# Chains of a gated delta rule that begin with queries and keys, with the values joining later, in a two-block fp32 kernel

## The chip, the core and the metric

The kernel runs on one core of a Trainium2 chip. TensorE (PE) multiplies, VectorE (DVE), ScalarE (ACT) and GpSimd (POOL) do the element-wise work, and SyncE (SP) issues the loads. The metric is the device time of one execution in microseconds (us); the time before is the median of three runs, and the changed kernel is timed in the same way.

## What is computed

Two transformer blocks run one after the other on 256 tokens of width 1024. The first block puts 16 meta tokens in front (272 rows in all), then has a layer with a gated delta rule and a layer with an mLSTM, each followed by a feed-forward part with a short convolution. The second block has a SwiGLU part, three mixers and another SwiGLU part. Only the delta rule is touched here:

```python
proj = h @ w_in
qkv = silu(causal_depthwise_conv(proj[..., :o1], conv_w))      # q 1024, k 1024, v 2048 columns
z = proj[..., o1:o2]                                           # 2048 columns
beta = sigmoid(...); g = -exp(a_log) * softplus(... + dt_bias) # 16 heads each
q = l2_normalize(q) * 128 ** -0.5;  k = l2_normalize(k)        # 8 heads, each serves 2 value heads
a_mat = eye + (k*beta) @ k^T * decay * strict                  # per head and chunk
u, w = solve(a_mat, [v*beta, k*beta*exp(G)])
v_new = u - w @ S;  o = (q*exp(G)) @ S + (q @ k^T * decay) @ v_new
S = S * gt + (k * exp(G_last - G))^T @ v_new                   # state from chunk to chunk
o = rms_norm(o) * silu(z);  out = o @ w_out
```

## The kernel before

Every fp32 product is split: an operand is cast to a high part (`wh`, `xhl`) and the rest (`wl`), and three matmuls are summed into a PSUM tile `ps`. A projection of 256 columns is 48 such matmuls over 272 tokens. The delta rule's layer has 16 projections for queries, keys and values in four groups (`gdn_proj`: keys, queries, two tiles of values for each group) and 8 projections `z`, 1152 matmuls in all. ACT empties each `ps` into `cx` and `cy`, and DVE runs the four-tap convolution as three instructions on `cy` (`conv4`). PSUM has two buffers for `ps`.

The rest of the layer is a chain for each pair of heads (8) and each of two chunks of 128 tokens, in four lanes at a time. `unit_kq` turns keys and queries to token rows (`kqp`), scales them to unit length with a short row of small DVE instructions (`rq_v`, `rq_y`, `rq_a`), ACT writes `kqtok`, and PE turns them back (shown as `kqp<-eye,kqtok`, called the back transposes below). `gdn_pre` builds the decays (`dp`, `BA`, `kk`) and, in the kernel before, the values as token rows times beta (`vp`, `bv`). `gdn_core` inverts a 128x128 triangular matrix in six doubling levels (`rtp`, then `yp` and `w` by turns, then `zp` and `r2p`; its tile is `RT`), and then forms `up`, `sp` and `op`, the state and the output. After four cores of a group the outputs are normed on DVE (`rq_o`, `on`) and turned by PE (`otp`). The last 16 tokens of all heads are one more chain (`gdn_tail`), which ends in `rsp`, in `r` and in the products `og` that the output projection reads.

The gates (`gdn_gates`: `psba`, `bap`, `lp`, `gg`, `gp`, `stk`, `rp`) are needed by every chain's decays. `residual` turns the input by 24 transposes `trx`.

A planner in the kernel (`Threads`) writes out the order of PE's instructions: each piece of work is a Python generator which yields the tiles and PSUM banks that its next step needs, or an event, and a number that is added as a wish for a later time. The planner keeps an estimated clock and always takes the first generator whose step is ready. PE runs exactly that order. The order on DVE, ACT and POOL comes from the scheduler of the tile framework. An engine executes its own list strictly in order, so an instruction that has to wait holds up all that stands behind it.

In the kernel before, the chunk-0 generator runs the gates first and then, group by group, `before(g, 0)`; the chunk-1 generator runs `before(g, 1)`. `before` waits for `proj_done[g]`, all four projections of the group. The functions that the change touches, and what calls them:

Of the kernel before, what the change touches and what calls it, by code (L numbers as in the profile page):

```python
# [208 lines left out]
class Kern:  # L209
# [664 lines left out]
    def residual(self):  # L874

        for k in range(KD):
            yield [f"p{k % 4}", 10.0 + 1.0 * k]
            self.lane = k % 4
            p = self.plane("trx", (128, T))
            for t, (o, P) in enumerate(TT):  # L880
                self.tr(p[:, o:o + P], self.xt[t][k // 4][:P, (k % 4) * 128:(k % 4) * 128 + 128], P)
            self.A.copy(self.hs[k], p[:])
# [107 lines left out]

    def gdn_proj(self, X, g):
        W = self.i["gdn_w_in"][0]
        qs, ks, v0, v1 = (self.vslot() for _ in range(4))
        for base, dst in ((1024 + g * 256, ks), (g * 256, qs), (2048 + g * 512, v0), (2304 + g * 512, v1)):
            yield from self.linear_g(W, base, 256, KD, X, T, lambda m, p: self.conv4(p, base // 128 + m, dst[:, m, :]))
        tl = slice(256, T)
        self.G.tensor_copy(self.kqtail[:, 0, 2 * g:2 * g + 2, :], ks[:, :, tl])
        self.G.tensor_copy(self.kqtail[:, 1, 2 * g:2 * g + 2, :], qs[:, :, tl])
        for n, v in enumerate((v0, v1)):
            self.G.tensor_copy(self.vtail[:, 4 * g + 2 * n:4 * g + 2 * n + 2, :], v[:, :, tl])  # L1000
        return qs, ks, (v0, v1)

    def unit_kq(self, x, c):


        n = len(x)
        yield list(x) + [f"pu{c}"]
        self.lane = f"u{c}"
        ss = self.tiny([128, n], "kqss")
        p = self.plane("kqp", (128, n, 128))  # L1010
        for h in range(n):
            self.tr(p[:, h, :], x[h])
        for h in range(n):
            self.square_sum(ss[:, h:h + 1], p[:, h, :])
        r = self.rsqrt_small([128, n], ss[:], 1.0, 4 * EPS)
        rq = r[:].rearrange("p (h e) -> p h e", e=2)[:, :, 1]
        self.ts(rq, rq, 128.0 ** -0.5, ALU.mult)
        kq = self.ring(f"kq{c}", "kqtok", (128, n, 128))
        for h in range(n):
            self.act(kq[:, h, :], p[:, h, :], AF.Copy, scale=r[:, h:h + 1])  # L1020
        yield [kq[:], f"pu{c}", 0.8]
        self.lane = f"u{c}"
        p2 = self.plane("kqp2", (128, n, 128))
        for h in range(n):
            self.tr(p2[:, h, :], kq[:, h, :])
        kqT = self.ring(f"kqT{c}", "kqT", (128, n, 128))
        self.A.copy(kqT[:], p2[:])
        return kq, kqT
# [88 lines left out]

    def gdn_pre(self, q, c, kqT, v):


        sl = slice(c * 128, c * 128 + 128)
        h0 = 2 * q
# [11 lines left out]
        BA = yield from self.decays(kqT[:, 0, :], kqT, diff, 0, self.nG[:, c, h0:h0 + 2])  # L1134
        yield [BA[:], f"pu{c}"]
        self.lane = f"u{c}"
# [4 lines left out]
        for h in range(2):  # L1141
            self.act(bv[:, h, :], vp[:, h, :], AF.Copy, scale=self.beta[:, c, h0 + h:h0 + h + 1])
        return BA, bv

    def gdn_core(self, q, c, kq, kqT, BA, bv, ss, state_of):

        h0 = 2 * q
        lane = self.lane = (q % 2) * 2 + c
        R2 = yield from self.wy_inverse(BA[:, 0], 2, 128)
        aT = BA[:, 1]  # L1150
        S_ = self.St[q]
# [164 lines left out]
    def gdn(self, X):  # L1316
# [6 lines left out]
        proj, state = {}, events(8)  # L1323
        proj_done, after_done = events(), events()
        pre, pre_one, core_done = {}, [events() for _ in range(4)], [events() for _ in range(4)]
# [6 lines left out]
        def projections():  # L1332
            todo, nz = list(range(4)), 0
            while todo or nz < 8:
                if todo and (todo[0] < 2 or all(ev.on for ev in pre_done[todo[0] - 2])):
                    g = todo.pop(0)
                    self.lane = None
                    proj[g] = yield from self.gdn_proj(X, g)
                    proj_done[g].set()
# [9 lines left out]
        def before(g, c):  # L1349
            yield proj_done[g]  # L1350
            qs, ks, vs = proj[g]
            for n in (c, 2 + c):
                if g > 1:
                    yield core_done[g - 2][n]
            u = yield from self.unit_kq([t[:, m, ch[c]] for m in range(2) for t in (ks, qs)], c)
            yield gates_done
            for m in range(2):
                j = 2 * g + m - 3
                if j >= 0:
                    yield core_done[j // 2][j % 2 * 2 + c]  # L1360
                kq, kqT = (t[:, 2 * m:2 * m + 2, :] for t in u)
                pre[g, 2 * m + c] = (kq, kqT) + (yield from self.gdn_pre(2 * g + m, c, kqT, vs[m]))
                pre_one[g][2 * m + c].set()
            pre_done[g][c].set()

# [7 lines left out]

        def first_chunks():
            yield from self.gdn_gates(X)
            gates_done.set()
            for g in range(4):
                yield from before(g, 0)
# [49 lines left out]

        self.th.add([lane(n) for n in range(4)] + [first_chunks(), second_chunks(), gating()])
        self.columns(self.convs, PV_GC)  # L1430
# [1017 lines left out]
```

## Time and profile before

| what | value |
| --- | --- |
| median of 3 runs | 1668.59 us (1667.01 to 1671.13) |
| the profiled execution's own time | 1671.11 us |
| its span from first to last instruction | 1669.3 us |
| TensorE busy | 1564.4 us, 94% of the span |
| VectorE busy | 1120.0 us, 67% |
| ScalarE busy | 927.9 us, 56% |
| GpSimd busy | 579.2 us, 35% |
| chain that ended last | PE 68%, DVE 22%, ACT 5%, DMA 3% |
| mean granted TensorE clock | 0.973 |

The shares are averages over the whole kernel. The delta rule's layer is the first quarter of it, up to about 379 us, and there the digits of the busy tenths of DVE are as high as 8 and PE's fall to 7 and 8. From the output projection on PE stands at 9 in most slices. A row of the timeline gives the start, the duration, the engine, the operation with its tiles, and in brackets how long the engine stood idle in front of it and who released it. Ends of matmuls are modelled, so spacing is read from start to start.

### The profile page before, as it was taken

How to read it: one execution, taken by the hardware profiler on the slowest of the kernel's cores; microseconds unless marked ns; L12 is line 12 of the kernel's file. 1: busy time of each engine (PE TensorE's matmuls, PEld its weight loads, DVE VectorE, ACT ScalarE, POOL GpSimd, SP SyncE). 2: the span in 40 equal slices, each digit the busy share in tenths (PEclk: the TensorE clock that was granted, in tenths of full speed). 3: DMA queues.
4: the chain of work that ended last, by engine and by line, in shares of the span. 5: the costliest groups of instructions: out<-in, count | busy, mean ns of one | idle time of the engine just before them, and what ended most of it. 6: DMA issues, size and time to landing. Idle time of an engine off the chain costs nothing.

```text
span 1669.3 us, 31255 instructions
## 1 busy us (share of the span) xinstructions
PE 1564.4 (94%) x11980; PEld 1475.4 (88%) x11980; DVE 1120.0 (67%) x2223; ACT 927.9 (56%) x1877; POOL 579.2 (35%) x535
## 2 busy tenths in 40 slices
PE   8889888899999998999899998999997899999999
PEld 6788778799899997888899998999985789999987
DVE  5788877766888757457877668464659663566643
ACT  4567767655566554446566556454553655564542
POOL 3574555320200002550344441122275548511221
PEclk9799999999999999999999999999998999999999
DMA  5331221226355554335366564566553335656564
GB/s 158 89 89 52 69 64 47 77 90 214 106 178 174 169 175 111 96 115 164 107 185 192 175 185 148 163 199 192 173 166 111 111 93 150 183 164 188 180 189 151
DMA packets 239100, 235.39 MB, mean 141 GB/s; under 512 B 11511, under 2 KB 226407, under 8 KB 238951
## 3 DMA queue, kind: packets, MB, share of 16 engines
q1 hardware_dynamic: 238326, 231.86, 46.4%
q8 instruction: 94, 1.54, 0.4%
q0 software_dynamic: 496, 1.41, 0.4%
q14 instruction: 56, 0.45, 0.1%
q10 hardware_dynamic: 128, 0.13, 0.0%
HBM read 232.32 MB, written 1.05 MB: 140 GB/s over the span
## 4 chain that ended last, share of the span: by engine, by line
PE 68%; DVE 22%; ACT 5%; DMA 3%; issue 2%; POOL 0%; ACTq 0%; POOLq 0%; DVEq 0%
PE ps L190 52%; PE pst L190 5%; DVE cy L190 3%; DVE rq_a L190 3%; ACT wh L190 2%; DVE RT L190 2%; DVE wl L190 1%; DVE rq_y L190 1%; PE memp L190 1%; DMA wraw<-in_ffn_w_up_dram 1%; DVE xn L190 1%; PE rsp L190 1%; DVE on L190 1%; PE w L190 1%; PE up L190 1%
## 5 line engine op out<-in xcount | busy, mean ns | idle before, releaser
L190 PE MATMUL ps<-xhl,wh 128*128 128x256 f32 (+2 forms) x4496 | 861.6, 294 | 28.9 <-DVE py L190 11.1
L190 PEld LDWEIGHTS ps<-xhl,wh 128*128 128x128 f32 x4496 | 703.0, 193 | 38.3 <-DVE py L190 6.9
L190 ACT CAST wh<-wraw 128x1024 fp32r<-128x1024 f32 (+2 forms) x436 | 448.0, 1029 | 389.8 <-PE ps L190 255.9
L190 PE MATMUL ps<-xhl,wl 128*128 128x256 f32 (+2 forms) x2248 | 626.0, 287 | 0.8 <-DVE wl L190 0.8
L383 POOL TENSOR_TENSOR wl<-wraw,wh 128x512 fp32r<-128x512 f32 (+3 forms) x264 | 334.7, 1291 | 658.2 <-ACT wh L190 622.8
L190 PEld LDWEIGHTS ps<-xhl,wl 128*128 128x128 f32 x2248 | 423.9, 192 | 1.0 <-DVE wl L190 1.0
L190 DVE TENSOR_TENSOR wl<-wraw,wh 128x1024 fp32r<-128x1024 f32 (+2 forms) x237 | 287.4, 1213 | 182.4 <-ACT wh L190 179.2
L190 POOL TENSOR_TENSOR wl<-wraw,wh 128x512 fp32r<-128x512 f32 x134 | 173.9, 1319 | 153.1 <-ACT wh L190 136.2
L190 PE MATMUL ps<-hh,wh 128*128 128x256 f32 (+1 forms) x1056 | 191.1, 283 | 0.0
L190 PEld LDWEIGHTS ps<-hh,wh 128*128 128x128 f32 x1056 | 163.2, 189 | 0.0
L190 PE MATMUL ps<-hh,wl 128*128 128x256 f32 (+1 forms) x528 | 149.7, 284 | 0.0
L190 DVE SCALAR_TENSOR_TENSOR fy<-ps,pvt,fy 128x256 f32<-128x256 f32 (+2 forms) x176 | 84.9, 488 | 25.1 <-ACT fy L190 23.2
L190 PEld LDWEIGHTS ps<-hh,wl 128*128 128x128 f32 x528 | 99.4, 188 | 0.0
L190 DVE SCALAR_TENSOR_TENSOR cy<-cx,pvt,cy 128x271 f32<-128x271 f32 (+2 forms) x96 | 74.5, 779 | 13.5 <-ACT cy L190 12.5
L190 DVE TENSOR_TENSOR hh<-fy,hh 128x256 fp32r<-128x256 f32 (+1 forms) x88 | 64.4, 735 | 13.2 <-ACT hh L190 12.8
L190 POOL MEMSET mvt<- 128x4 f32 x4 | 0.4, 102 | 176.0 <-PE ps L190 176.0
L190 ACT ACTIVATE fy<-ps,pvt 128x272 f32<-128x272 f32 (+1 forms) x88 | 49.5, 568 | 12.3 <-PE ps L190 11.8
L190 DVE TENSOR_TENSOR py<-ps,rstd 128x256 f32<-128x256 f32 x72 | 29.9, 420 | 37.9 <-PE ps L190 37.9
L190 PE MATMUL pst<-wh,hh 128*128 128x512 f32 x176 | 55.1, 394 | 0.0
L190 ACT CAST hh<-fy 128x256 fp32r<-128x256 f32 (+1 forms) x88 | 35.7, 407 | 29.8 <-DVE fy L190 29.0
L190 DVE CAST_PREDICATED RT<-lvl,w 128x512 f16<-128x512 uint8 x67 | 44.9, 683 | 7.1 <-PE w L190 6.8
L190 PE MATMUL ps<-og,wh 128*128 128x272 f32 x256 | 48.6, 289 | 0.1
(523 smaller groups left out, 2420.4 us busy)
## 6 DMA issues: line engine op xcount, KB each, us to landing
wraw<-in_ffn_w_up_dram SPq DMA_DIRECT2D x88, 512.0 KB
wraw<-in_ffn_w_gu_dram SPq DMA_DIRECT2D x88, 512.0 KB
wraw<-in_ffn_w_down_dram SPq DMA_DIRECT2D x79, 512.0 KB
wraw<-in_gdn_w_in_dram SPq DMA_DIRECT2D x48, 512.0 KB
wraw<-in_w_in_dram SPq DMA_DIRECT2D x41, 512.0 KB
wraw<-in_ml_w_in_dram SPq DMA_DIRECT2D x24, 512.0 KB
wraw<-in_gdn_w_out_dram SPq DMA_DIRECT2D x16, 512.0 KB
wraw<-in_ml_w_out_dram SPq DMA_DIRECT2D x8, 512.0 KB
```

The costliest lines, as they stand in the source:

```text
L190: r = f(*args, **kw)
L383: eng.tensor_tensor(l[:, a, b], r[:, a, b], h[:, a, b].bitcast(F32), ALU.subtract)
```

## The change

Keys and queries of a group set an event `kq_done` as soon as their two projections are issued, and `before` waits for that in place of `proj_done`. `gdn_pre` ends with the decays; a new function `gdn_values` makes the value rows, and `gdn_core` waits for them by an event behind its inverse. For group 0 both pairs' decays come first and both pairs' values after them; for later groups values follow each pair's decays. The gates become a generator of their own, in front of the chunk-0 generator, so that the first scaling (group 0, chunk 0, now in the PSUM bank of lane 0) no longer stands behind them. `residual` asks for its transposes later (26 us and 1.5 us apiece, no longer 10 and 1), and no longer names its PSUM bank.

```diff
--- before.py
+++ after.py
@@ -874,7 +874,7 @@
     def residual(self):
 
         for k in range(KD):
-            yield [f"p{k % 4}", 10.0 + 1.0 * k]
+            yield [26.0 + 1.5 * k]
             self.lane = k % 4
             p = self.plane("trx", (128, T))
             for t, (o, P) in enumerate(TT):
@@ -988,11 +988,13 @@
         else:
             self.stt(out, th[:], 1.0, y[:], ALU.add, ALU.mult)
 
-    def gdn_proj(self, X, g):
+    def gdn_proj(self, X, g, kq_done):
         W = self.i["gdn_w_in"][0]
         qs, ks, v0, v1 = (self.vslot() for _ in range(4))
         for base, dst in ((1024 + g * 256, ks), (g * 256, qs), (2048 + g * 512, v0), (2304 + g * 512, v1)):
             yield from self.linear_g(W, base, 256, KD, X, T, lambda m, p: self.conv4(p, base // 128 + m, dst[:, m, :]))
+            if dst is qs:
+                kq_done.set((qs, ks))
         tl = slice(256, T)
         self.G.tensor_copy(self.kqtail[:, 0, 2 * g:2 * g + 2, :], ks[:, :, tl])
         self.G.tensor_copy(self.kqtail[:, 1, 2 * g:2 * g + 2, :], qs[:, :, tl])
@@ -1000,12 +1002,13 @@
             self.G.tensor_copy(self.vtail[:, 4 * g + 2 * n:4 * g + 2 * n + 2, :], v[:, :, tl])
         return qs, ks, (v0, v1)
 
-    def unit_kq(self, x, c):
+    def unit_kq(self, x, c, lane=None):
 
 
         n = len(x)
-        yield list(x) + [f"pu{c}"]
-        self.lane = f"u{c}"
+        lane = f"u{c}" if lane is None else lane
+        yield list(x) + [f"p{lane}"]
+        self.lane = lane
         ss = self.tiny([128, n], "kqss")
         p = self.plane("kqp", (128, n, 128))
         for h in range(n):
@@ -1018,8 +1021,8 @@
         kq = self.ring(f"kq{c}", "kqtok", (128, n, 128))
         for h in range(n):
             self.act(kq[:, h, :], p[:, h, :], AF.Copy, scale=r[:, h:h + 1])
-        yield [kq[:], f"pu{c}", 0.8]
-        self.lane = f"u{c}"
+        yield [kq[:], f"p{lane}", 0.8]
+        self.lane = lane
         p2 = self.plane("kqp2", (128, n, 128))
         for h in range(n):
             self.tr(p2[:, h, :], kq[:, h, :])
@@ -1115,8 +1118,7 @@
         self.tt(e[:], kk[:, :, None, :].to_broadcast([128, 2, 2, 128]), e[:], ALU.mult)
         return e
 
-    def gdn_pre(self, q, c, kqT, v):
-
+    def gdn_pre(self, q, c, kqT):
 
         sl = slice(c * 128, c * 128 + 128)
         h0 = 2 * q
@@ -1132,7 +1134,13 @@
                     self.mm(d[:, kind, h, :], selc(kind, h), rw, kind == 0 and h == 0, False)
 
         BA = yield from self.decays(kqT[:, 0, :], kqT, diff, 0, self.nG[:, c, h0:h0 + 2])
-        yield [BA[:], f"pu{c}"]
+        return BA
+
+    def gdn_values(self, q, c, v):
+
+        sl = slice(c * 128, c * 128 + 128)
+        h0 = 2 * q
+        yield [v[:], f"pu{c}"]
         self.lane = f"u{c}"
         vp = self.plane("vp")
         bv = self.ring(f"bv{c}", "bv")
@@ -1140,13 +1148,15 @@
             self.tr(vp[:, h, :], v[:, h, sl])
         for h in range(2):
             self.act(bv[:, h, :], vp[:, h, :], AF.Copy, scale=self.beta[:, c, h0 + h:h0 + h + 1])
-        return BA, bv
-
-    def gdn_core(self, q, c, kq, kqT, BA, bv, ss, state_of):
+        return bv
+
+    def gdn_core(self, q, c, kq, kqT, BA, values, ss, state_of):
 
         h0 = 2 * q
         lane = self.lane = (q % 2) * 2 + c
         R2 = yield from self.wy_inverse(BA[:, 0], 2, 128)
+        yield values
+        bv = values.v
         aT = BA[:, 1]
         S_ = self.St[q]
         if c:
@@ -1321,7 +1331,8 @@
         ch = [slice(c * 128, c * 128 + 128) for c in range(2)]
         events = lambda n=4: [Event() for _ in range(n)]
         proj, state = {}, events(8)
-        proj_done, after_done = events(), events()
+        proj_done, after_done, kq_done = events(), events(), events()
+        values = {(g, n): Event() for g in range(4) for n in range(4)}
         pre, pre_one, core_done = {}, [events() for _ in range(4)], [events() for _ in range(4)]
         pre_done = [events(2) for _ in range(4)]
         gates_done, tail_pre, tail_done, gating_done, norm_ready = events(5)
@@ -1335,7 +1346,7 @@
                 if todo and (todo[0] < 2 or all(ev.on for ev in pre_done[todo[0] - 2])):
                     g = todo.pop(0)
                     self.lane = None
-                    proj[g] = yield from self.gdn_proj(X, g)
+                    proj[g] = yield from self.gdn_proj(X, g, kq_done[g])
                     proj_done[g].set()
                 elif nz < 6 or not todo:
                     if nz == 6:
@@ -1347,20 +1358,28 @@
                     yield from pre_done[todo[0] - 2]
 
         def before(g, c):
-            yield proj_done[g]
-            qs, ks, vs = proj[g]
+            yield kq_done[g]
+            qs, ks = kq_done[g].v
             for n in (c, 2 + c):
                 if g > 1:
                     yield core_done[g - 2][n]
-            u = yield from self.unit_kq([t[:, m, ch[c]] for m in range(2) for t in (ks, qs)], c)
+            u = yield from self.unit_kq([t[:, m, ch[c]] for m in range(2) for t in (ks, qs)], c, None if g or c else 0)
             yield gates_done
             for m in range(2):
                 j = 2 * g + m - 3
                 if j >= 0:
                     yield core_done[j // 2][j % 2 * 2 + c]
                 kq, kqT = (t[:, 2 * m:2 * m + 2, :] for t in u)
-                pre[g, 2 * m + c] = (kq, kqT) + (yield from self.gdn_pre(2 * g + m, c, kqT, vs[m]))
+                BA = yield from self.gdn_pre(2 * g + m, c, kqT)
+                pre[g, 2 * m + c] = kq, kqT, BA, values[g, 2 * m + c]
                 pre_one[g][2 * m + c].set()
+                if g:
+                    yield proj_done[g]
+                    values[g, 2 * m + c].set((yield from self.gdn_values(2 * g + m, c, proj[g][2][m])))
+            if not g:
+                yield proj_done[g]
+                for m in range(2):
+                    values[g, 2 * m + c].set((yield from self.gdn_values(2 * g + m, c, proj[g][2][m])))
             pre_done[g][c].set()
 
         def after(g):
@@ -1371,9 +1390,11 @@
                 yield from self.gdn_onorm(on[g, n], r[:, n, :], self.oT[2 * g + n // 2][:, :, ch[n % 2]])
             after_done[g].set()
 
-        def first_chunks():
+        def gates():
             yield from self.gdn_gates(X)
             gates_done.set()
+
+        def first_chunks():
             for g in range(4):
                 yield from before(g, 0)
                 if g == 0:
@@ -1426,7 +1447,7 @@
                     split(len(Y) - 1, slice(0, 256))
             gating_done.set()
 
-        self.th.add([lane(n) for n in range(4)] + [first_chunks(), second_chunks(), gating()])
+        self.th.add([lane(n) for n in range(4)] + [gates(), first_chunks(), second_chunks(), gating()])
         self.columns(self.convs, PV_GC)
         yield from projections()
         yield from [tail_done, after_done[3]] + core_done[3]
```

The built orders show the rest. No instruction is added or taken away on TensorE but for how rows group; from the output projection on, the orders of all engines are the same in both kernels, and so is the order of the 1152 projection matmuls among themselves. What moves is where the chains' steps stand between them. Three places follow.

On VectorE, at the end of the gates' chain (`gg` is the tile that `gp` on TensorE waits for, `cy` a tap of the convolution of the first queries):

```order
 L190 SCALAR_TENSOR_TENSOR gg<-ba,lp 128x48
 L190 SCALAR_TENSOR_TENSOR lb<-ba,lp 128x48
+L190 SCALAR_TENSOR_TENSOR cy<-cx,pvt,cy 128x271
 L190 SCALAR_TENSOR_TENSOR gg<-gg,al 128x48
-L190 SCALAR_TENSOR_TENSOR cy<-cx,pvt,cy 128x271
 L190 TENSOR_SCALAR beta<-beta 128x48
 L190 SCALAR_TENSOR_TENSOR cy<-cx,pvt,cy 128x270
+L190 SCALAR_TENSOR_TENSOR cy<-cx,pvt,cy 128x269
 L190 COPY Gc<-gp 128x16 x2
 L190 COPY Gc<-gp 16x16
-L190 SCALAR_TENSOR_TENSOR cy<-cx,pvt,cy 128x269
```

One tap moved in front of the last step of the gates, and another in front of the copies of `gp`.

On VectorE, at the first scaling of group 0 (`rq_v` is its first step for each of the two chunks):

```order
 L190 SCALAR_TENSOR_TENSOR cy<-cx,pvt,cy 128x270
 L190 SCALAR_TENSOR_TENSOR cy<-cx,pvt,cy 128x269
-L190 SCALAR_TENSOR_TENSOR cy<-cx,pvt,cy 128x271
-L190 SCALAR_TENSOR_TENSOR cy<-cx,pvt,cy 128x270
-L190 SCALAR_TENSOR_TENSOR cy<-cx,pvt,cy 128x269
-L190 SCALAR_TENSOR_TENSOR cy<-cx,pvt,cy 128x271
-L190 SCALAR_TENSOR_TENSOR cy<-cx,pvt,cy 128x270
-L190 SCALAR_TENSOR_TENSOR cy<-cx,pvt,cy 128x269
 L190 TENSOR_SCALAR rq_v<-kqss 128x4
 L190 TENSOR_SCALAR rq_y<-rq_v 128x4
```

The six taps of the second tile of values no longer stand in front of the scaling; they follow it. On TensorE `kqp` stands behind 144 projection matmuls, where it stood behind 192, the back transposes behind 195 (246 before), the first `rtp` behind 222 (288 before).

On VectorE, at the end of the tail chain, before the change (`r` is the tail's norm, `zs` the gate, `og` the operand of the output projection, `wl` the low part of one of its weights):

```order
L190 TENSOR_TENSOR r<-up,r 128x256
L190 TENSOR_TENSOR zs<-oT,zs 128x2x256
L190 TENSOR_TENSOR zs<-r,zs 128x2x16 x7
L190 SCALAR_TENSOR_TENSOR og<-zs,gw,og 128x2x16 x2
L190 SCALAR_TENSOR_TENSOR og<-zs,gw,og 128x2x256
```

And after it:

```order
L190 TENSOR_TENSOR zs<-oT,zs 128x2x256
L190 TENSOR_TENSOR r<-up,r 128x256
L190 TENSOR_TENSOR zs<-r,zs 128x2x16 x7
L190 TENSOR_TENSOR wl<-wraw,wh 128x1024
L190 SCALAR_TENSOR_TENSOR og<-zs,gw,og 128x2x16 x3
```

A subtraction for a weight moved in front of the first `og`. On TensorE 33 projection matmuls stand between `rsp` and the first product with `og`, 48 before. On ScalarE the first of the two table loads stands behind `sq` and one `og`; before, it stood behind `sq`, a cast of a weight, a `zth` and the copy of the last `otp`.

## Rows read from the trace of the kernel before

**Rows 1.** Windows: start:end, us; then PE, PEld, DVE, ACT, POOL busy; PEclk, DMA, GB/s
```profile
19.00:379.00 360.00, 312.52 (x2536) 285.42 (x2536) 276.60 (x656) 231.09 (x682) 181.14 (x196) 0.93 0.26 76
379.00:1669.30 1290.30, 1234.36 (x9368) 1179.89 (x9366) 833.47 (x1524) 687.07 (x1176) 393.68 (x323) 0.98 0.53 158
```

**Rows 2.** Waits of TensorE from 18 to 380 us: total, times, longest
```profile
PE yp L190 <- DVE RT L190: 13.7, 10, 3.3
PE kqp L190 <- ACT kqtok L190: 6.7, 4, 3.5
PE gp L190 <- DVE gg L190: 5.2, 1, 5.2
PE otp L190 <- DVE on L190: 5.0, 3, 4.4
PE zp L190 <- DVE RT L190: 4.8, 5, 2.2
```

**Rows 3.** Timeline of TensorE, a residual transpose in front of the gates' `gp`
```profile
37.71 0.54 PE L190 MATMUL trx<-eye,xt 128*128 128x128 f32 x3
```

**Rows 4.** Timeline of VectorE behind the gates' last step
```profile
44.28 0.49 DVE L190 SCALAR_TENSOR_TENSOR cy<-cx,pvt,cy 128x271 f32<-128x271 f32 x1
44.69 0.18 DVE L190 TENSOR_SCALAR beta<-beta 128x48 f32<-128x48 f32 x1
```

**Rows 5.** Timeline of TensorE, first scaling of group 0
```profile
66.34 1.04 PE L190 MATMUL kqp<-eye,kv 128*128 128x128 f32 x8
...
75.92 0.52 PE L190 MATMUL ps<-xhl,wh 128*128 128x272 f32 x2 [1.02 <-ACT cy L190]
...
81.05 1.11 PE L190 MATMUL kqp<-eye,kqtok 128*128 128x128 f32 x4 [3.54 <-ACT kqtok L190]
```

**Rows 6.** Timeline of VectorE in the same stretch
```profile
59.34 6.88 DVE L190 SCALAR_TENSOR_TENSOR cy<-cx,pvt,cy 128x271 f32<-128x271 f32 x6 [2.46 <-ACT cy L190]
67.44 7.13 DVE L190 SCALAR_TENSOR_TENSOR cy<-cx,pvt,cy 128x271 f32<-128x271 f32 x6 [1.22 <-ACT cy L190]
74.49 0.16 DVE L190 TENSOR_SCALAR rq_v<-kqss 128x4 f32<-128x4 f32 x1
...
75.98 1.19 DVE L190 SCALAR_TENSOR_TENSOR rq_a<-rq_y 128x4 f32<-128x4 f32 x1
...
82.96 3.23 DVE L190 SCALAR_TENSOR_TENSOR cy<-cx,pvt,cy 128x271 f32<-128x271 f32 x3 [0.94 <-ACT cy L190]
...
89.47 1.29 DVE L190 TENSOR_TENSOR BA<-kk,BA 128x512 f32<-128x512 f32 x2 [1.99 <-PE kk L190]
```

**Rows 7.** Timeline of GpSimd in the same stretch
```profile
65.89 2.71 POOL L190 TENSOR_TENSOR wl<-wraw,wh 128x512 fp32r<-128x512 f32 x2
...
73.30 0.97 POOL L190 TENSOR_TENSOR cth<-cth,cy 128x272 f32<-128x272 f32 x1
74.66 2.49 POOL L190 TENSOR_TENSOR wl<-wraw,wh 128x512 fp32r<-128x512 f32 x2 [0.39 <-ACT wh L190]
```

**Rows 8.** Timeline of TensorE: steps of an inverse, then two thirds of two projection triples
```profile
337.63 0.28 PE L190 MATMUL w<-Y,RT 128*128 128x128 f16 x2
337.75 0.28 PE L190 MATMUL w<-RT,Y 128*128 128x128 f16 x2
...
364.19 0.41 PE L190 MATMUL ps<-xhl,wh 128*128 128x272 f32 x2
...
364.57 0.42 PE L190 MATMUL ps<-xhl,wh 128*128 128x272 f32 x2
```

**Rows 9.** Timeline of TensorE at the end of the layer
```profile
361.10 0.60 PE L190 MATMUL rsp<-sq,ones 128*128 128x256 f32 x2
...
368.32 0.56 PE L190 MATMUL ps<-og,wh 128*128 128x272 f32 x2
```

**Rows 10.** Timeline of ScalarE at the same place
```profile
362.62 1.28 ACT L190 ACT_TABLE_LOAD   x1
363.92 0.47 ACT L190 ACTIVATE r<-rsp,epst 128x256 f32<-128x256 f32 x1
```

## The prediction

> **What bounds the kernel now.** I read the page first: TensorE is busy for 94% of the span, so time can only be lost or won where it stands idle or runs at its lower clock. The windows come next [rows 1]. Behind 379 us TensorE is busy for 1234.4 of 1290.3 us, and the built orders of all engines are the same there in both kernels; I give that part no change. The delta rule's layer, 19 to 379 us, takes 360.0 us with 312.5 busy: 47.5 us of idle time, and a granted clock of 0.93, so that about a seventh of this stretch passes at 1.2 GHz. The same matmuls run after the change, so the whole question is how much of these 47.5 us the new order keeps. The list of TensorE's waits names most of them [rows 2]: 13.7 us in front of `yp` and 4.8 us in front of `zp`, both for VectorE's part of the inverse, 6.7 us for the scaled keys and queries, 5.2 us once for the gates, and 5.0 us for the normed outputs. VectorE ends nearly all of these, and it is busy for 276.6 of the 360.0 us. So the layer is bound by TensorE with VectorE close behind, and TensorE loses wherever its fixed order reaches a chain's step before VectorE has finished it. The reader is to see that no wait stands at the layer's very end: filling matmuls run up to the first `og` [rows 9].
>
> A projection matmul costs 0.125 us: three of them lie between two starts 0.38 us apart [rows 8]. A step of the inverse costs 0.06 us a matmul, two in 0.12 us [rows 8].
>
> **The change part by part.** The sum is a difference against the profiled execution (1671.11 us, span 1669.3 us and 1.8 us around it). That execution lies 2.5 us above the median of the runs shown, 1668.59 us, to which I apply the difference.
>
> *Gates.* VectorE runs a tap of the convolution in front of the last step of the gates; from its start to the next start are 0.41 us [rows 4]. TensorE has one transpose of `residual` less to do in front of `gp`, 0.54 us [rows 3]; that work comes back later. So `gp` starts 0.4 us later with 0.5 us less done: plus 0.9 us, between 0.4 (the transpose fills a later wait) and 1.5 (both fall into the half-speed stretch behind the wait).
>
> *First scaling.* Before, `kqp` starts at 66.34 us behind 192 matmuls, and the back transposes start at 81.05 us after a wait of 3.54 us [rows 5]. Afterwards `kqp` stands 48 matmuls earlier, 6.0 us, of which the later gates and a further transpose take back about 1: some 61.3 us. From there TensorE needs about as long as before to the back transposes, 10.2 us without the wait of 1.02 us between them: it arrives at 71.5 us. On VectorE `rq_v` no longer stands behind the second six taps (67.44 to 74.49 us), only behind the first six, which end at 66.2 us [rows 6]. If the rest takes the 6.56 us from `rq_v` to the back transposes that it took before, the tile is there at 72.8 us, and the wait shrinks to 1.3 us: minus 2.2 us. But GpSimd works without a pause from 65.9 to 74.3 us, seven instructions in the rows cited by first and last [rows 7], and small instructions beside it are slow: an `rq_a` took 1.19 us where `rq_v` took 0.16 [rows 6]. Before, the scaling met four such GpSimd instructions; with seven, three more instructions lose 1.0 us each, and the wait is 4.4 us: plus 0.9 us. I take the middle, minus 0.6 us.
>
> The Trainium skill, SBUF — State Buffer, section "Who interferes with whom", says that a DVE instruction with two SBUF inputs contends with a GpSimd instruction that reads SBUF, while one with a single SBUF input does not. Here the trace agrees for the taps: 1.19 us on average beside GpSimd [rows 6], 0.49 us for a tap that met none of it [rows 4]. By that rule the upper bound of this step, plus 0.9 us, would be the likelier end.
>
> *The inverses.* Chains of group 0 start 66 matmuls earlier on TensorE (8.2 us). VectorE stands idle for 1.22, 0.94 and 1.99 us between 66 and 90 us, because taps wait for projections and the first `BA` waits for `kk` [rows 6]. After the change the taps of the second value tile, which are ready, lie in that stretch behind the scaling, so I let these 4.15 us go, and since VectorE ends TensorE's waits behind it, I pass them on one for one: minus 4.1 us. The order supports the direction: counting TensorE's other work between the steps of each inverse at the prices above, the 80 gaps from `w` to the next `yp` grow from 2.56 to 2.94 us on average, and the 16 inverses from 527.8 to 558.5 us in all, 7.7 us a lane. It also shows the danger: the 16 gaps from `w` to `zp` shrink from 2.26 to 1.75 us. Bounds: minus 13.7 us (no `yp` waits any more) and plus 8.7 us (each of 17 `zp`, the tail's with them, waits 0.51 us longer and nothing else gets better). I take minus 4.1, nearest to the idle rows.
>
> *Values.* `vp` and `bv` keep their count. They are asked for between a third and a half of an inverse ahead of `up`, so their wait costs nothing; the inverse of some 30 us covers it. If that cover went, a core would stand still for an ACT instruction of 256 elements, 0.47 us by the nearest row [rows 10]. The event adds a wait only to the planner, not to an engine. SP's queue keeps its loads in order; the only difference is that four loads for a later stage stand side by side, behind all weights of this layer's projections. Cost 0, between minus 0.5 and plus 0.5 us.
>
> *Normed outputs.* Four sets of `otp` stand 36 to 54 matmuls behind the last `op` of their group, where they stood 39 to 57 behind. The longest wait there, 4.4 us [rows 2], belongs to group 1, whose distance falls from 57 to 36. Yet the other two of the three waits share only 0.6 us, with distances of 39 and 42, so distance does not decide. Cost 0, between minus 5.0 (the waits go) and plus 2.6 us (21 matmuls of cover gone).
>
> *End of the layer.* Before, `rsp` starts at 361.10 us and ends at 361.70, and the first `og` product starts at 368.32: 6.6 us, which 48 matmuls (6.0 us) and a short wait fill [rows 9]. Afterwards 33 matmuls fill 4.1 us. The chain itself gets shorter: the first table load began 0.9 us behind `rsp` and let `r` start at 363.92 [rows 10]; it now stands behind less and can be nearly over when `rsp` ends, an estimate of 1.7 us saved, while a subtraction in front of `og` takes about 0.3 back. 6.6 - 1.7 + 0.3 = 5.2 against 4.1: plus 1.1, taken as 1.0 us. Bounds: minus 0.5 (the short wait goes too) and plus 2.5 us (the chain is as long as before).
>
> Sum: 0.9 - 0.6 - 4.1 + 0 + 0 + 1.0 = minus 2.8 us, so 1665.8 us.
>
> **The rivals.** *The last level gets too little cover* (slower). The six-level inverse ends in copies on ACT and VectorE, and TensorE now comes to `zp` 0.51 us sooner. For it: `zp` waited already, 4.8 us in five places [rows 2]. Against it: twelve of 17 did not wait. If all 17 pay, 8.7 us; the ten waits at `yp`, each up to 0.38 us shorter, give 3.8 back; with 0.9 for the gates, 1.0 for the end and minus 0.6 for the scaling this is plus 6.2 us, 1674.8 us. It decides from a mean wait of about 0.7 us in front of `zp` on.
>
> *VectorE pays at GpSimd* (no change). The scaling lands in the stretch where GpSimd never pauses [rows 7], loses the 3.1 us above, and that eats most of the 4.15 us of idle time. For it: the slow taps [rows 6]. Against it: GpSimd's work has to be met by some instruction anyway. 0.9 + 0.9 - 1.0 + 1.0 = plus 1.8 us, 1670.4 us. It is what the Trainium skill's rule on the shared port (SBUF — State Buffer, "Who interferes with whom") would mean here.
>
> *The lead does not last* (no change; the change does not do what it says). The order shows it for one group: the `r2p` of group 1 stand behind 579 to 618 matmuls, 561 to 648 before, though group 0 led by 66. Against it: groups 2 and 3 lead again, 711 to 792 against 780 to 816. Without the minus 4.1 the sum is plus 1.3 us, 1669.9 us.
>
> *The slack is worth more* (faster). If the 7.7 us a lane shorten the waits in full, the scaling gains its 2.2 us and `otp` 2.0, then 0.9 - 2.2 - 7.7 - 2.0 + 1.0 = minus 10.0 us, 1658.6 us. For it: the waits in rows 2 come to 35.4 us, and each also costs time at the half clock behind it. Against it: the larger gaps are a few of 5 to 8 us, the median gap is 2.14 us in both orders.
>
> **How the numbers follow.** What a measurement of this kernel can tell from no change is about 0.3%, 5.0 us. Forecast 0.52, with a range of its own from 1661 to 1670 us; of it 0.20 faster by more than 0.3%, 0.32 within. More slack 0.19, all but 0.01 of it faster. GpSimd 0.08 and no lasting lead 0.07, both within. Too little cover 0.14, nearly all slower. Together: faster 0.38, within 0.48, slower 0.14. The range from 1658 to 1674.5 us takes in the larger gain and most of the loss.
>
> **What would show it.** Right: the wait for `gp` at about 6 us; the back transposes of group 0 at about 73 to 75 us with a wait below 3.5; VectorE without idle time of a microsecond between 66 and 90 us; less than 13.7 us in front of `yp`; a wait of about 1 us in front of the first `og`; the layer's end near 376 us. Wrong: more than 10 us in front of `zp`, single scaling instructions above 1 us all through the first scaling, a stretch behind the output projection that differs by over 1 us, or the layer's end at 379 us or later.

## The result: slower by 1.56%, and the profile after

The changed kernel takes 1695.18 us (median of 4 runs, 1691.10 to 1699.28) against 1667.81 us before (4 runs, 1667.01 to 1671.13). The ratio is 1.0156, 95% interval 1.0136 to 1.0176: 27 us slower, outside the predicted range of 1658 to 1674.5 us. The profiled execution of after took 1699.28 us, the slowest of its four, with a span of 1697.5 us. Of all the runs that follow, one, of the kernel with PLAG 0.64 below, took 2248 us at a granted clock of 0.61 and is left out of its median.

The windows come first. Both kernels are cut at their first projection matmul of the layer and at their first `og` product; columns as in [rows 1]. Before:

```profile
24.01:368.32 344.31, 298.28 (x2437) 272.44 (x2437) 263.84 (x629) 221.38 (x664) 181.14 (x196) 0.94 0.25 73
368.32:1669.28 1300.96, 1244.91 (x9449) 1190.12 (x9447) 843.99 (x1547) 695.99 (x1193) 393.68 (x323) 0.98 0.53 158
```

After:

```profile
22.12:389.61 367.49, 302.74 (x2439) 276.68 (x2437) 252.76 (x629) 224.05 (x664) 180.28 (x196) 0.92 0.24 70
389.61:1697.45 1307.84, 1250.77 (x9447) 1195.80 (x9447) 847.18 (x1548) 696.23 (x1192) 394.31 (x323) 0.98 0.52 157
```

Length less TensorE's busy time is its idle time: 46.0 us before, 64.8 us after. So 18.7 of the layer's 23.2 us more are idle time; the rest is the same work done longer, with a granted clock of 0.92 where it was 0.94. Behind the first `og` the list of instructions is the same, and 6.9 us more there come with 5.9 us more of busy time.

TensorE's waits of after, 18 to 420 us (total, times, longest), against [rows 2]:

```profile
PE yp L190 <- DVE RT L190: 21.4, 14, 5.0
PE trx L190 <- ACT kqtok L190: 9.0, 1, 9.0
PE otp L190 <- DVE on L190: 7.7, 3, 3.2
PE gp L190 <- DVE gg L190: 6.3, 1, 6.3
PE kqp L190 <- ACT kqtok L190: 5.8, 2, 5.5
...
PE zp L190 <- DVE RT L190: 1.3, 1, 1.3
```

A line is new: a `trx` of `residual` waits 9.0 us for the scaled keys, with which it has no data in common. TensorE's timeline of after, which answers to [rows 5]:

```profile
56.68 1.04 PE L190 MATMUL kqp<-eye,kv 128*128 128x128 f32 x8
...
66.72 0.90 PE L190 MATMUL trx<-eye,xt 128*128 128x128 f32 x3 [9.00 <-ACT kqtok L190]
...
72.08 0.54 PE L190 MATMUL trx<-eye,xt 128*128 128x128 f32 x3
...
77.00 0.60 PE L190 MATMUL kqp<-eye,kqtok 128*128 128x128 f32 x4
```

and VectorE's, against [rows 6]:

```profile
61.73 0.72 DVE L190 TENSOR_SCALAR rq_v<-kqss 128x4 f32<-128x4 f32 x1
...
76.12 2.05 DVE L190 SCALAR_TENSOR_TENSOR cy<-cx,pvt,cy 128x271 f32<-128x271 f32 x3 [9.93 <-ACT cy L190]
```

`residual` takes lanes 0 to 3 by turns. The first scaling now holds lane 0's bank until ACT has written `kqtok`, and the `trx` of k = 4 stands right behind `kqp` on TensorE and wants that bank. The diff removed the bank's name from the wait, so the planner could not see it. TensorE stands still, no projection feeds VectorE, which then idles 9.93 us, and the three `trx` behind the stop take 0.90 us where 0.54 is usual: from 66.72 to 70.40 us, behind the standstill, TensorE's granted clock is 0.51, which is the 1.2 GHz level.

The longest wait at `yp`, 5.04 us, shows what such a wait is made of. TensorE's row, and then what VectorE did meanwhile:

```profile
261.07 0.39 PE L190 MATMUL yp<-RT,Br 128*128 128x128 f16 x2 [5.04 <-DVE RT L190]
```

```profile
257.27 1.21 DVE L190 SCALAR_TENSOR_TENSOR rq_y<-rq_a,rq_y 128x4 f32<-128x4 f32 x1
258.51 1.19 DVE L190 SCALAR_TENSOR_TENSOR rq_a<-rq_y 128x4 f32<-128x4 f32 x1
...
260.79 0.22 DVE L190 CAST RT<-w 32x64 f16<-32x64 f32 x1
```

VectorE does not stand idle. Its own fixed list has another chain's scaling and a tap of the convolution in front of the last copy of `RT`, and two of these small instructions last over a microsecond each beside GpSimd.

### The profile page after: what moved, and what is told of

It is laid out like the page before. It is cut to its first block, busy times and chain, and to the rows that moved or that the text cites. A ratio compares the mean times of both kernels' runs of the same rounds, so it can differ in the third digit from the quotient of the medians.

```text
span 1697.5 us, 31222 instructions
## 1 busy us (share of the span) xinstructions
PE 1572.8 (93%) x11980; PEld 1484.4 (87%) x11980; DVE 1112.1 (66%) x2223; ACT 930.8 (55%) x1877; POOL 578.8 (34%) x535
## 3 DMA queue, kind: packets, MB, share of 16 engines
HBM read 232.32 MB, written 1.05 MB: 137 GB/s over the span
## 4 chain that ended last, share of the span: by engine, by line
PE 69%; DVE 19%; ACT 6%; DMA 3%; issue 2%; POOL 1%; ACTq 0%; POOLq 0%; DVEq 0%
PE ps L190 54%; PE pst L190 4%; DVE cy L190 3%; DVE rq_a L190 2%; ACT wh L190 2%; DVE wl L190 1%; DVE RT L190 1%; DVE rq_y L190 1%; PE memp L190 1%; PE w L190 1%; DVE xn L190 1%; PE rsp L190 1%; DMA wraw<-in_ml_w_out_dram 1%; DVE xhl L190 1%; PE up L190 1%
## 5 line engine op out<-in xcount | busy, mean ns | idle before, releaser
L190 PE MATMUL ps<-xhl,wh 128*128 128x256 f32 (+2 forms) x4496 | 868.2, 295 | 27.8 <-DVE py L190 10.3
L190 DVE SCALAR_TENSOR_TENSOR cy<-cx,pvt,cy 128x271 f32<-128x271 f32 (+2 forms) x96 | 67.7, 705 | 26.3 <-ACT cy L190 25.1
L190 ACT ACTIVATE fy<-ps,pvt 128x272 f32<-128x272 f32 (+1 forms) x88 | 49.6, 568 | 13.6 <-PE ps L190 13.0
```

The source lines that it names most:

```text
L190: r = f(*args, **kw)
```

## The experiments

Four theories. One: the shared bank costs nearly everything, since a stop of 9 us spoils the timing of the fixed order behind it. Two: the earlier chains cost the rest. Three: the later place of `residual`'s transposes does. Four, formed after the first four runs: the order before is a point at which the planner's constants happen to fit, and any new deal of it costs the layer waits (a deal is one of the orders that the planner gives out). Each ratio is against runs of the kernel before on the same chip; "idle" is TensorE's, from the first projection to the first `og` of the profiled run, worked out as above.

| kernel | median us | ratio (95%) | idle us |
| --- | --- | --- | --- |
| before | 1667.8 | 1 | 46.0 |
| after | 1695.2 | 1.0156 (1.0136 to 1.0176) | 64.8 |
| A free bank | 1689.8 | 1.0118 (1.0097 to 1.0139) | 57.7 |
| B own bank | 1701.2 | 1.0189 (1.0171 to 1.0206) | 65.7 |
| C before, `residual` later | 1685.7 | 1.0094 (1.0080 to 1.0109) | 55.6 |
| D chains alone | 1694.5 | 1.0136 (1.0115 to 1.0158) | 58.1 |
| before, PLAG 0.66 | 1678.7 | 1.0057 (1.0044 to 1.0070) | 53.8 |
| before, PLAG 0.64 | 1682.8 | 1.0068 (1.0049 to 1.0087) | 54.5 |
| before, KC 0.81 | 1686.9 | 1.0107 (1.0089 to 1.0124) | 52.9 |
| before, KC 0.85 | 1685.5 | 1.0106 (1.0085 to 1.0128) | 57.8 |
| before, KC 0.75 | 1679.8 | 1.0062 (1.0043 to 1.0081) | 51.3 |
| before, SAME 0.14 | 1691.2 | 1.0140 (1.0124 to 1.0156) | 56.9 |
| before, PLAG 0.70 | 1691.6 | 1.0138 (1.0124 to 1.0151) | 56.8 |
| A, KC 0.85 | 1686.5 | 1.0093 (1.0074 to 1.0112) | 59.4 |
| A, KC 0.75 | 1684.5 | 1.0098 (1.0067 to 1.0129) | 59.4 |
| A, SAME 0.14 | 1680.8 | 1.0065 (1.0048 to 1.0081) | 53.2 |
| A, PLAG 0.70 | 1684.1 | 1.0093 (1.0069 to 1.0117) | 59.3 |
| A, SAME 0.12 | 1688.4 | 1.0108 (1.0086 to 1.0129) | 59.1 |
| A, back transposes later | 1694.0 | 1.0138 (1.0118 to 1.0157) | 59.2 |
| E bank named | 1704.0 | 1.0203 (1.0188 to 1.0218) | 66.3 |

**A, free bank.** After, in which `residual` leaves bank 0 alone; TensorE's list stays the same.

```diff
-            self.lane = k % 4
+            self.lane = 1 + k % 3
```

> The kernel after, in which residual takes its PSUM banks as 1, 2, 3, 1, ... and never 0, the bank of the first unit scaling; TensorE's order is the same, instruction by instruction. Theory one (the transposes of residual that stand behind the kqp of the first scaling wait for the bank that the scaling still holds, and this one stop costs the layer its timing): the 9.0 us wait of trx goes, and with it at least 13 us of the 27 us, so 1682 us or less, perhaps down to 1668. Theory two (the bank costs its own 9 us and no more; the earlier chains themselves cost the rest): the wait goes and the time falls by 9 to 10 us only, to about 1686. Theory three (the later place of residual's transposes costs the time): no fall beyond the wait, as in theory two, 1686.

The wait is gone. TensorE's timeline of A:

```profile
56.83 1.04 PE L190 MATMUL kqp<-eye,kv 128*128 128x128 f32 x8
57.70 0.54 PE L190 MATMUL trx<-eye,xt 128*128 128x128 f32 x3
...
69.72 0.82 PE L190 MATMUL ps<-xhl,wh 128*128 128x272 f32 x2 [3.52 <-ACT cy L190]
...
70.57 1.06 PE L190 MATMUL kqp<-eye,kqtok 128*128 128x128 f32 x4
```

ScalarE's in the same stretch:

```profile
67.86 1.14 ACT L190 ACTIVATE kqtok<-kqp,rq_y 128x128 f32<-128x128 f32 x4 [3.35 <-DVE rq_y L190]
...
69.14 0.53 ACT L190 ACTIVATE cy<-ps,pvt 128x272 f32<-128x272 f32 x1
```

and its window and main waits:

```profile
22.25:379.62 357.37, 299.64 (x2438) 273.86 (x2436) 255.16 (x628) 224.34 (x664) 180.36 (x196) 0.94 0.25 71
```

```profile
PE yp L190 <- DVE RT L190: 21.4, 14, 5.0
PE otp L190 <- DVE on L190: 7.7, 3, 3.3
PE gp L190 <- DVE gg L190: 6.3, 1, 6.3
PE kqp L190 <- ACT kqtok L190: 6.1, 3, 5.5
```

The layer is 10.1 us shorter than that of after (357.37 for 367.49), but the profiled run of A is the fastest of its six (1682.03 us) and that of after the slowest of its four. By the ratios the bank costs 0.0038, 6 us, with about 5 us either way from the two intervals. The median of 1689.8 us lies above all three forecasts. So much of theory one is shown; its knock-on is not: `yp` 21.4, `otp` 7.7 and `gp` 6.3 are the lines of after to a tenth. 20 us stay. Part of the stop comes back in another form, 3.52 us for `cy`: ScalarE stands 3.35 us for `rq_y` in front of `kqtok`, and the `cy` that frees a buffer for TensorE stands behind `kqtok` in its list.

**B, own bank.** After, with the first scaling in the chunk's own bank.

```diff
-            u = yield from self.unit_kq([...], c, None if g or c else 0)
+            u = yield from self.unit_kq([...], c)
```

> The kernel after, with the first unit scaling in its own bank as before the change (it waits for the gates' chain then); the rest of the change stands. Theory one (the shared bank costs the time): no wait of 9 us at trx, and 1665 to 1675 us. Theory two (earlier chains cost the rest): about 1686 us. Theory three (the later transposes of residual): about 1686 us, with waits at trx or behind it.

**C, only `residual`.** The kernel before with `residual`'s new line.

```diff
-            yield [f"p{k % 4}", 10.0 + 1.0 * k]
+            yield [26.0 + 1.5 * k]
```

> The kernel before, with only the new line of residual (its transposes due later and the bank's name gone); nothing of the delta rule is moved. Theory one: no scaling holds bank 0 in that stretch, so no long wait at trx, and 1666 to 1670 us. Theory two: as theory one. Theory three (the later transposes cost the time by themselves): 1680 us or more.

**D, chains alone.** After, with `residual`'s old line and the own bank of B.

```diff
-            yield [26.0 + 1.5 * k]
+            yield [f"p{k % 4}", 10.0 + 1.0 * k]
```

> The kernel after, with residual's line as before and the first scaling in its own bank: what is left of the change is that chains begin when keys and queries are convolved, and that the values join behind the inverse. Theory one (the shared bank is the cause): 1662 to 1672 us. Theory two (the earlier chains cost some 17 us themselves): 1680 to 1688 us. Theory three (residual): 1662 to 1672 us, and the second kernel of this set slow.

B and D missed theory one's forecasts by 26 and 22 us or more, though no `trx` waits in B (its largest waits are 15.1 us at `kqp` for `kqtok` and 13.6 us at `ps` for `zs`), and D is slower than theory two allowed. C came out as theory three has it, but that theory wanted D, which keeps the old `residual`, at 1672 us or less. The pieces do not add up: C (15.5 us over its before) and D (24.4 us) make 39.9 us, B, which holds both, costs 31.1. Nor do the waits repeat. C has its loss at `yp`; D, in which `yp` waits less than in before, has it at `kqp` and `zp`. C's waits:

```profile
PE yp L190 <- DVE RT L190: 22.7, 15, 4.7
PE otp L190 <- DVE on L190: 7.0, 2, 3.9
```

D's:

```profile
PE kqp L190 <- ACT kqtok L190: 15.7, 8, 4.1
PE zp L190 <- DVE RT L190: 8.8, 5, 5.1
PE yp L190 <- DVE RT L190: 6.1, 7, 3.5
```

That a different wait pays each time is what led to theory four.

**Neutral deals of the order before.** Three constants of the planner's clock are moved here: KC (a factor on the estimated cost of the other engines), SAME and PLAG (lags behind an operand). Moving one by a hundredth changes nothing of the computation, only which step the planner takes first.

```diff
-        self.th.KC, self.th.LAG, self.th.SAME, self.th.PLAG = 0.8, 0.25, 0.18, 0.65
+        self.th.KC, self.th.LAG, self.th.SAME, self.th.PLAG = 0.8, 0.25, 0.18, 0.66
```

> The kernel before, with one constant of the planner's cost model 0.01 us larger in this layer (PLAG 0.66 for 0.65): nothing of the delta rule is changed, but the built order of TensorE differs behind group 1. Theory four (the order before is a point at which the planner's constants happen to fit, and any new deal of the order costs the layer 10 to 25 us of waits and half clock, whatever the edit): 1678 to 1692 us. Rival, theory two with theory three (the edits themselves put steps into bad places): a neutral new deal costs nothing on average, so 1666 to 1674 us.

The second is KC 0.81, the third PLAG 0.64:

> The kernel before, with the planner's factor on the costs of the other engines at 0.81 for 0.80: a second neutral new deal, which differs from group 0 on. Theory four: 1678 to 1692 us. Theories two and three: 1666 to 1674 us.

> The kernel before with PLAG 0.64 for 0.65, a step to the other side of the neutral change that cost 9.4 us. Theory four (the constants of before are a point that fits; both sides of it are worse): 1676 to 1688 us. Rival (a smooth dependence: less lead assumed is better or the same): 1660 to 1670 us.

All three are slower than before, by 9.4, 17.6 and 13.5 us, and for PLAG on both sides of the constant. The first shows it in the trace. TensorE's timeline with PLAG 0.66:

```profile
77.52 1.12 PE L190 MATMUL kqp<-eye,kqtok 128*128 128x128 f32 x4 [3.54 <-ACT kqtok L190]
...
123.03 0.29 PE L190 MATMUL yp<-RT,Br 128*128 128x128 f16 x2 [3.30 <-DVE RT L190]
...
176.06 0.40 PE L190 MATMUL yp<-RT,Br 128*128 128x128 f16 x2 [5.89 <-DVE RT L190]
```

and of before:

```profile
126.34 0.40 PE L190 MATMUL yp<-RT,Br 128*128 128x128 f16 x2 [3.30 <-DVE RT L190]
...
177.43 0.22 PE L190 MATMUL zp<-RT,Br 128*128 128x128 f16 x1 [1.72 <-DVE RT L190]
```

Up to 123 us the two run alike: the same waits of 3.54 and 3.30 us, 3.5 and 3.3 us apart because the profiled run of before came that much later out of the first 45 us (its `gp` starts at 44.42 us, 41.13 here). From there the lists differ, and at 176 us one of them meets a `yp` whose `RT` is 5.89 us late. VectorE works meanwhile; its list has six scalings of normed outputs and three taps in front of that `RT`:

```profile
170.37 3.43 DVE L190 TENSOR_SCALAR on<-on,rq_o 128x128 f32<-128x128 f32 x6
...
174.45 1.30 DVE L190 SCALAR_TENSOR_TENSOR cy<-cx,pvt,cy 128x270 f32<-128x270 f32 x3
175.79 0.22 DVE L190 CAST RT<-w 32x64 f16<-32x64 f32 x1
```

No work was added; the two fixed lists only meet less well at that step.

**Deals of the changed order.** A with KC 0.85, KC 0.75, SAME 0.14 and PLAG 0.70, and A with the back transposes asked for 1.6 us behind their operands (`yield [kq[:], f"p{lane}", 1.6]` for 0.8):

> The kernel after with residual in banks 1 to 3 (as in the first experiment, 1689.8 us) and the planner's factor at 0.85 for 0.80, so that it reckons with slower engines and leaves more between the steps. Theory four: the time lies anywhere between 1670 and 1695 us, and the waits in front of yp and kqp change places. Theory two (the earlier chains cost the time): within 5 us of 1689.8 us, or above.

> As the last, with the factor at 0.75: the planner reckons with faster engines, so TensorE comes to each step sooner and the layer's chains end about 63 projection matmuls sooner (rsp behind 1056 matmuls, not 1119). Theory four: anywhere between 1670 and 1700 us, more in front of yp, zp and kqp, nothing in front of the first og. Theory two: within 5 us of 1689.8 us, or above.

> The kernel after with residual in banks 1 to 3 and the planner's constant for one step behind another on the same engine at 0.14 for 0.18: chains are placed sooner (rsp behind 1077 matmuls for 1119). Theory four: 1672 to 1695 us. Theory two (earlier chains cost the time): above 1690 us.

> The kernel after with residual in banks 1 to 3 and the planner's lag to TensorE at 0.70 for 0.65: chains are placed with more lead. Theory four: 1672 to 1692 us. Theory two (earlier chains cost the time, more lead changes little): 1684 to 1692 us.

> The kernel after with residual in banks 1 to 3, and the back transposes of the unit scaling asked for 1.6 us later than their operands instead of 0.8, since the longest wait left in group 1 stands there (5.5 us). Theory four: the wait at kqp shrinks to under 3 us, but other waits change with the new deal; 1672 to 1692 us. Theory two: 1684 to 1690 us, the waits at kqp apart.

They lie between 1680.8 and 1694.0 us. SAME 0.14 brings the chains of group 0 on still sooner and is 9 us faster, which is against theory two; KC 0.85 and PLAG 0.70 lie in the ranges of both theories, and KC 0.75 only 0.3 us outside theory two's, so these three do not tell. The last one, at 1694.0 us, lies above both forecasts. It aimed at one wait and missed: `kqp` fell only from 6.1 to 6.0 us, while its `zp` rose from 1.3 to 8.6 us:

```profile
PE yp L190 <- DVE RT L190: 15.4, 12, 3.1
PE zp L190 <- DVE RT L190: 8.6, 5, 2.8
...
PE kqp L190 <- ACT kqtok L190: 6.0, 3, 4.1
```

**Pairs at equal constants.** What the change itself costs, with the fit lost on both sides:

> The kernel before with the planner's factor at 0.85; its pair with the change (bank 0 left free) took 1686.5 us. Theory four (a new deal costs the time, the change itself about nothing): 1680 to 1692 us, the mean of the four pairs' differences within 4 us of zero. Theory two (the change itself costs most): 1668 to 1676 us, the change slower by 10 us or more in each pair.

> The kernel before with the planner's factor at 0.75; its pair with the change took 1684.5 us. Theory four: 1678 to 1692 us. Theory two: 1668 to 1675 us.

> The kernel before with the planner's same-engine step at 0.14; its pair with the change took 1680.8 us. Theory four: 1676 to 1690 us. Theory two: 1665 to 1672 us.

> The kernel before with the planner's lag to TensorE at 0.70; its pair with the change took 1684.1 us. Theory four: 1678 to 1692 us. Theory two: 1668 to 1675 us.

The kernel before lands where theory four had it in each, but for SAME 0.14, which is a microsecond above. Changed less unchanged, by medians: +1.0, +4.7, -10.3 and -7.5 us, mean -3 us; by the ratios, each against before on the same chip, the mean is -4 us. From their scatter four such differences fix the mean to about 11 us either way (an estimate). The layer of the kernel before with SAME 0.14, and then that of A with it:

```profile
22.96:384.96 362.00, 305.08 (x2437) 279.02 (x2437) 265.81 (x639) 226.25 (x671) 183.16 (x196) 0.92 0.24 71
```

```profile
22.63:376.83 354.20, 300.96 (x2438) 274.65 (x2437) 255.58 (x639) 227.59 (x673) 181.91 (x196) 0.93 0.25 72
```

Over all, the seven neutral deals of before have a mean ratio of 1.0097, the seven deals of A (itself among them) 1.0102. By the scatter of the two sevens, these means are equal to within some 6 us either way (an estimate). Theory two falls, and theory three with it, since A holds the later `residual`: apart from the bank, the change costs nothing that these runs can tell, and theory four accounts on average for some 16 us (0.0097) of the 27. In the profiles of the seven neutral deals the layer is 14.1 us longer on average than in before; 8.8 us of that are idle time, and the rest is the same work done longer, with a granted clock of 0.90 to 0.95 (before 0.94).

**E, bank named; and one more step of SAME.**

```diff
             yield [26.0 + 1.5 * k]
+            yield [f"p{k % 4}"]
             self.lane = k % 4
```

> The kernel after, in which residual keeps its four banks and names the one it wants in a second wait, so that the planner knows when it comes free: its last four transposes then stand behind 198 projection matmuls, behind the scaling's back transposes. If the shared bank costs what the free bank saved: no wait at trx, and the time like that of the first experiment or another new deal, 1680 to 1693 us. If the bank costs more than that: below 1680 us. If the stop only moves to another place: 1694 us or more.

> The kernel after with residual in banks 1 to 3 and the same-engine step at 0.12. If a smaller step is a slope (1689.8 us at 0.18, 1680.8 at 0.14): 1672 to 1679 us. If each constant is only another deal (theory four): anywhere from 1678 to 1695 us.

E moved the stop, as its last case says. TensorE's timeline of E:

```profile
68.95 3.40 PE L190 MATMUL trx<-eye,xt 128*128 128x128 f32 x12 [3.85 <-ACT kqtok L190]
...
73.81 1.05 PE L190 MATMUL kqp<-eye,kqtok 128*128 128x128 f32 x4
```

and VectorE's:

```profile
63.45 1.27 DVE L190 TENSOR_SCALAR rq_v<-kqss 128x4 f32<-128x4 f32 x1
64.64 0.15 DVE L190 TENSOR_TENSOR rq_a<-rq_a,rq_v 128x4 f32<-128x4 f32 x1
64.76 1.19 DVE L190 TENSOR_SCALAR rq_y<-rq_v 128x4 int32<-128x4 int32 x1
```

and GpSimd's:

```profile
63.42 2.50 POOL L190 TENSOR_TENSOR wl<-wraw,wh 128x512 fp32r<-128x512 f32 x2
```

Two VectorE instructions of four elements a row last as long as one GpSimd instruction each (1.27 and 1.19 us beside 1.25), and the one between them 0.15. The Trainium skill, SBUF — State Buffer, "Who interferes with whom", says that `tensor_scalar` can take the shared port, and that the engine that comes second is then blocked for the other's whole instruction; these rows agree. The prediction's short form, that a single SBUF input does not contend, left this case out; in before too an `rq_y` of this kind took 1.26 us beside GpSimd (at 74.69 us). The planner now knows the bank, but four sets of `trx` still queue up together in front of the back transposes, not behind them as was expected, and come 3.85 us before the bank is free. SAME 0.12 gave 1688.4 us: no slope below 0.14. No deal tried beats the kernel before. B and E, 31 and 34 us over it, lie above every neutral deal (9 to 24 us); what costs them the difference was not tested.

## Why the prediction was wrong, point by point

- *First scaling*, the step that failed first: "From there TensorE needs about as long as before to the back transposes, 10.2 us". It needed 20.3 us (56.68 to 77.00). 9.0 us of that is the bank, a wait that the term put at nothing, though the diff shows both halves of it, the bank's name going and the scaling coming to lane 0; about 1 us more is the lower clock behind the stop. The rest of the term held. Without the bank (A) the stretch takes 13.7 us, 10.2 of them work, as forecast, and 3.52 a wait, which is the old wait for the scaled keys, met through ScalarE's `cy`. Before, the two waits of the stretch came to 4.56 us [rows 5], so A gains 1.0 us there where 0.6 was forecast.
- *Inverses*, the step that failed by most: "since VectorE ends TensorE's waits behind it, I pass them on one for one: minus 4.1 us". VectorE's idle time did not go (9.93 us in one piece), and in A, without that piece, `yp` waits 21.4 us against 13.7. With `zp` (1.3 us, 4.8 before) the waits of the inverse rose by 4.2 us, inside the term's bounds but with the other sign. The mean gap from `w` to `yp` grows in the order, by the prediction's count from 2.56 to 2.94 us, but the wait is paid at single steps where VectorE's list has other work in front of `RT` (5.04 us at one `yp` of after), and a mean over 80 gaps of TensorE's list does not show these.
- The frame of the sum failed with it. It took the 47.5 us of idle time as what any order has, of which edits add and remove pieces. The runs show that before is no neutral base: it had the least idle time of all 20 kernels (46.0; the others 51.3 to 66.3), and seven of seven deals without any edit cost 9 to 24 us. So a new order had to be priced at about plus 16 us first, a mean that only these runs gave, and its edits after; with the bank's 6 us that is 22 of the 27. The last 5 lie within the scatter of the deals (plus 9 to 24 us). The sum also had no term of its own for the clock, which is the 4.5 us of the layer's 23.2 that are not idle time.
- *Gates*, plus 0.9 us: right; the wait for `gp` went from 5.2 to 6.3 us.
- *Values*, 0: right; no wait for them is among TensorE's.
- *Normed outputs*, 0, bounds minus 5.0 to plus 2.6: the waits rose by 2.7 us, just past the upper bound.
- *End of the layer*, plus 1.0 us: right for the first `og`, which waits 1.30 us; the second waits another 1.05 us, which was not foreseen. Both stay within the upper bound of 2.5.
- *Behind the layer*, no change: 6.9 us more in the profiled run, at the same list, 0.4 us less in A's. Of the 6.9, 5.9 are busy time of the same list, so clock and not order; the rest is about the wait of the second `og`.
- The rival on the slower side had the sign, not the mechanism: `zp` waits 1.3 us in after, 4.8 before. The rival of VectorE at GpSimd is real in size (1.27 us for an `rq_v` in E, 0.16 in [rows 6]) and reaches `yp` too, as the 5.04 us show. It is still not what the change added: the 117 instructions that write or read `rq_a` take 33.6 us in the layer before and 34.3 after. The rival of more slack held that each wait costs time at the half clock behind it; not each does. Around two `yp` waits of 1.6 us in before (190 to 200 and 295 to 300 us) the granted clock is 1.00, around the one of 3.30 us (125 to 130 us) it is 0.66.

What stays open is why the order before fits so well. Its constants may have been picked by timing, or it is luck; no run tells, and a deal of the changed kernel that fits as well was neither found nor ruled out.

## What to carry to other kernels

Where a planner writes a fixed order for engines that run in order, a tuned kernel is one deal out of many, and an edit is judged against other deals: build a few with a constant moved by a hundredth, on both sides, before a reason is given to a structure. When a wait's list of names gets shorter in a diff, look up who holds that buffer at the new place, since the hardware will still wait for it. A mean of the slack says little; look for the few steps that come first, and for what the other engine's list has in front of them.

## What the runs showed of the chip that was not expected

The stretch behind the first `og` has the same instructions in all kernels, and still took 1298.4 us in one profiled run and 1308.6 us in another, with TensorE busy for 1244.9 and 1252.3 us: the lower clock fell on different stretches. Two of its rows, before with SAME 0.14 and then before with KC 0.81:

```profile
384.96:1683.32 1298.36, 1244.93 (x9449) 1190.98 (x9447) 837.60 (x1536) 692.56 (x1184) 394.51 (x323) 0.99 0.51 158
```

```profile
378.70:1687.25 1308.55, 1252.25 (x9447) 1195.89 (x9447) 843.49 (x1545) 694.08 (x1189) 393.61 (x323) 0.98 0.52 156
```

A single profile can so be 10 us off for reasons outside the layer that is studied; that is why the verdicts above rest on medians and the mechanisms on waits.
